# A transformer layer on one core: the state-space parameter chain placed between u's four projections, its loads put on three queues, and the attention mask filled by VectorE

## Chip, cores and metric

The kernel runs on one core of one Trainium2 chip. The metric is the device time of one launch in microseconds (us). Engines are TensorE (PE; its weight loads are shown as PEld), VectorE (DVE), ScalarE (ACT), GpSimd (POOL) and SyncE (SP, which here only issues DMAs). A "q" behind an engine's name is its instruction queue, from which it issues DMAs too.

## The reference, cut to what matters

One layer on 1024 tokens of width 1024, in float32:

```
proj = x @ w_in                      -> q | k | v | u, each 1024 x 512
a = differential attention(q, k, v)  4 heads, two score maps each, softmax over chunks of 64:
                                     token t sees keys of chunks <= its own chunk
s = diagonal complex state space on u: 32 groups x 16 channels, 64 states each
    lam_bar = exp(lam * exp(log_dt)); b_bar = (lam_bar - 1) / lam * b; y = Re(c h) + d u
    then gelu and a gated unit (w_glu)
h = LayerNorm(alpha x + [a, s] @ w_out)
y = LayerNorm(alpha h + mixture of 32 experts, two per token)
```

The parameters of the state space (a, log_dt, b, c) need a chain of small elementwise work before the first group of u can be used: exponentials, a sine and cosine, powers of lam_bar, and the rotated b and c.

## The kernel before

Float32 products are made from two float32r parts, a high part (ACT casts) and the rest (DVE subtracts), so that one projection of 128 output columns is 48 matmuls of 128x512 (`proj`, L221): three for each of eight k tiles and two token halves. Its weights go through one raw buffer (`load_w`, L188, an SP load into the area `misc`), then `split_w` (L209) makes two pairs of parts in the tiles wa and wb in turn. A projection's result is a pair of PSUM banks, of which there are two.

The order of the program is:

- x is loaded in eight parts on SP (L194 to L197, w_in's column tile 12 after the fourth), turned on PE and split (`turn_x`, L199).
- u's four projections, column tiles 12 to 15 (L264), each written to `u_dram` and read back as `UT` by eight SP loads (`proj_u`, L244).
- The parameter chain, L268 to L526: eleven small loads into `a_in`, `ea` and `lamv` on ACT's queue (L376 to L384); `a_in` is turned on PE (`pa`, L390) and copied to `aa` (L393); then two exponentials (`vexp`), sine and cosine (`vsincos`), the powers LR and LI (L410 to L428), the factors CR and CI, the squares UC and US (L448 to L458), all on DVE; b loaded (L467 to L470) and rotated into BB1 and BB2; c loaded (L484 to L486), turned (`pc`, L490) and negated into CA and CB; and the tables pl and ph (`phases`, L499). B's four and cin's four loads are on ACT's queue.
- Eight units of four groups (`ssm_pair`, L636). `ssm_prepare(u)` (L543) makes X (three GpSimd operations), turns it on PE (`pk`, `pw`, L566 and L567), and makes M and C on GpSimd and Sn on DVE. X has one buffer. `ssm_unit` (L595) runs the scan. Behind each unit stands one of the projections q0 to q3, v0 to v3 as filler for PE.
- k's four projections, then attention by 32 pairs (head, block of 128 queries), two started ahead (L893). `scores` (L772) makes for each of two maps the score products (L781, L782), adds the mask, takes the maximum (DVE, L792 or L799) and the exponential (ACT, L786); `weigh` (L803) combines the two maps on DVE and multiplies by v on PE (L815, L819).
- The mask: `negr` (1x128: -1e30 for the first 64 query rows, 0 for the others) times `oner` (1x64 of ones), added to the last 64 keys by one matmul with one contraction row (L783), for every map of every pair: 64 in all.
- The output product `mix` (L1071), routing, and 32 experts from L1337 on.

What sets the order: the framework schedules before the run. Each engine has one queue that runs in order. The framework fills these queues with a model of time of its own, and among the instructions whose inputs that model has ready it takes the one that stands first in the program; so the place in the program is a priority, and an instruction may stand in its queue before one that is earlier in the program. From the first expert's gather on, the program's own order is kept (`keep_order`, L1309). A tile that takes another's place in memory waits until the earlier one is done with: the tiles come from 25 slots handed out in turn (`Slots`). B1 gets the slot of one of x's raw tiles. `pa` is a tile of the PSUM bank that x's turns use as well (`bank`, L131).

Of the kernel before, what the change touches and what calls it, by code (L numbers as in the profile page):

```python
# [11 lines left out]
F32 = mybir.dt.float32  # L12
F32R = mybir.dt.float32r
# [6 lines left out]
P = 128  # L20
# [5 lines left out]
NG = 32  # L26
# [88 lines left out]
def tile_kernel(ctx: ExitStack, tc: tile.TileContext, I: dict, out: bass.AP, dbg=None):  # L115
# [9 lines left out]
    sl = Slots()  # L125
# [62 lines left out]
    def load_w(ct):  # L188
# [2 lines left out]
        SP.dma_start(r, w_in[:, ct * P:(ct + 1) * P].rearrange("(k p) n -> p k n", p=P))  # L191
        wraw[ct] = r

    for t_ in range(NT):  # L194
        SP.dma_start(xraw[t_ // 2][:, t_ % 2, :], x2[t_ * P:(t_ + 1) * P, :])
        if t_ == WPOS:
            load_w(12)  # L197
# [46 lines left out]
    def proj_u(c4):  # L244

        o = proj(12 + c4)
        ut = sl.get([P, 8, P], F32, f"ut{c4}")
        for half in range(2):
            S.copy(ut[:, :, half * 64:half * 64 + 64],
                   o[:, half * 512:half * 512 + 512].rearrange("p (b s) -> p s b", s=8))  # L250
        SP.dma_start(u_dram[c4], ut)
        sl.put(ut)
        if c4 % 2 == 0:
            UTs[c4 // 2] = sl.get([P, 2, 8, P], F32, f"UT{c4}")
        UT = UTs[c4 // 2][:, c4 % 2, :, :]
        for s_ in range(8):
            tau = 7 - s_
            SP.dma_start(UT[16 * tau:16 * tau + 16],
                         u_dram[c4].rearrange("(g c) s b -> s c g b", c=16)[s_])
# [1 line left out]
    UTs, zT, qr, vv = {}, {}, {}, {}  # L261


    for c4 in range(4):  # L264
        proj_u(c4)


    spp = Area(sl, 2, "ssmp")  # L268
    tmpp = Area(sl, 4, "ssmt")
    n_tmp = [0]  # L270
    KEPT = ("mag", "LR", "LI")

# [100 lines left out]
        return so, co  # L373


    a_in = tmpp.get("a_in", [4, 64], parts=NG)  # L376
    for j in range(2):
        PQ.dma_start(a_in[:, j, :], I["ssm_a_re"][0])
        PQ.dma_start(a_in[:, 2 + j, :], I["ssm_a_im"][0])
    ea = small(NG + 2, "ea", keep=True)  # L380
    PQ.dma_start(ea[:, 0:NG], I["ssm_log_dt"][0].partition_broadcast(P))
    lamv = tmpp.get("lamv", [4, 64])
    for j, nm in enumerate(("lam_q1", "lam_k1", "lam_q2", "lam_k2")):
        PQ.dma_start(lamv[:, j, :], I[nm][0].partition_broadcast(P))  # L384
    lamp = tmpp.get("lamp", [2, 64])
    mul(lamp, lamv[:, 0::2, :], lamv[:, 1::2, :])
    V.tensor_reduce(out=ea[:, NG:NG + 2], in_=lamp, axis=AX.X, op=ALU.add)
# [74 lines left out]

    BB1 = bigp("BB1", [P, NG, 16])
    BB2 = bigp("BB2", [P, NG, 16])
    B1 = sl.get([P, 4, 512], F32, "B1")
    b1, b2, b3, b4 = (B1[:, j, :].rearrange("p (g c) -> p g c", c=16) for j in range(4))
    PQ.dma_start(b1[0:64], I["ssm_b_re"][0].rearrange("g p c -> p g c"))  # L467
    PQ.dma_start(b1[64:P], I["ssm_b_im"][0].rearrange("g p c -> p g c"))
    PQ.dma_start(b2[0:64], I["ssm_b_im"][0].rearrange("g p c -> p g c"))
    PQ.dma_start(b2[64:P], I["ssm_b_re"][0].rearrange("g p c -> p g c"))  # L470
    ts(b2[0:64], b2[0:64], -1.0, ALU.mult)
    CRb = CR.unsqueeze(2).broadcast_to([P, NG, 16])
    CIb = CI.unsqueeze(2).broadcast_to([P, NG, 16])
# [6 lines left out]
    sl.put(B1)  # L480
    CA = bigp("CA", [P, NG, 16])
    CB = bigp("CB", [P, NG, 16])
    cin = sl.get([P, 2, 4, 2, 64], F32, "cin")
    for v, pair in enumerate((("ssm_c_re", "ssm_c_im"), ("ssm_c_im", "ssm_c_re"))):  # L484
        for j, nm in enumerate(pair):
            PQ.dma_start(cin[:, v, :, j, :], I[nm][0].rearrange("(t g) c p -> (g c) t p", t=4))  # L486
    for v, dst in ((0, CA), (1, CB)):
        pc = bank(f"pc{v}")
        for t_ in range(4):
# [35 lines left out]
    dump("CB", CB)  # L525
    dump("nlam", nlam)  # L526

    tmpp.close()

    areas = [Area(sl, 1, f"ssm{j}") for j in range(5)] + [misc]  # L530
# [151 lines left out]
    kk = {}  # L682
# [57 lines left out]
                sl.put(wgh, wgl, gl_["raw"])  # L740


    negr = cp.tile([1, P], F32R, name="negr")
    G.memset(negr.bitcast(F32)[:, 0:64], -1e30)
    G.memset(negr.bitcast(F32)[:, 64:P], 0.0)
    oner = cp.tile([1, 64], F32R, name="oner")
    G.memset(oner.bitcast(F32), 1.0)
    mhalf = cp.tile([P, 4], F32, name="mhalf")
    G.memset(mhalf, -0.5)
    gcol = cp.tile([P, 1], F32, name="gcol")  # L750
# [21 lines left out]
    def scores(h, i, qd, L, j):  # L772
        n = P * (i + 1)
        tk = slice(i * P, (i + 1) * P)
        p_ = sl.get([P, 2, T], F32, f"p{h}_{i}")
        nm = sm("nm", 2)

        def products(s_, c):
            for c0 in range(0, n, 512):
                w = min(512, n - c0)  # L780
                PE.matmul(s_[:, c0:c0 + w], qd[0][:, c, tk], kk[h][:, c, c0:c0 + w], start=True, stop=False)  # L781
                PE.matmul(s_[:, c0:c0 + w], qd[1][:, c, tk], kk[h][:, c, c0:c0 + w], start=False, stop=c0 + w < n)  # L782
            PE.matmul(s_[:, n - 64:n], negr, oner, start=False, stop=True)  # L783

        def weights(s_, c):
            S.activation(p_[:, c, 0:n], s_[:, 0:n], AF.Exp, bias=nm[:, c:c + 1], accum_out=L[:, j, c:c + 1])  # L786

        if n <= 512:
            s2 = bank2(f"s{h}_{i}").rearrange("p (c n) -> p c n", c=2)
            for c in range(2):  # L790
                products(s2[:, c, :], c)
            V.tensor_reduce(out=nm, in_=s2[:, :, 0:n], axis=AX.X, op=ALU.max, negate=True)  # L792
            for c in range(2):
                weights(s2[:, c, :], c)
        else:
            for c in range(2):
                s_ = bank2(f"s{h}_{i}_{c}")
                products(s_, c)
                V.tensor_reduce(out=nm[:, c:c + 1], in_=s_[:, 0:n], axis=AX.X, op=ALU.max, negate=True)  # L799
                weights(s_, c)  # L800
        return p_
# [720 lines left out]
```

## Time and profile before

| | |
|---|---|
| Median of 3 runs | 1197.9 us (1195.63 to 1200.3) |
| The profiled execution | 1199.21 us, span 1197.5 us |
| PE busy | 1078.5 us, 90% of the span |
| DVE busy | 972.9 us, 81% |
| ACT busy | 704.2 us, 59% |
| POOL busy | 358.3 us, 30% |
| Chain that ended last | PE 62% of the span, DVE 5%, DMA 2% |

The stages are, by the times at which their lines run: x and u 0 to 64 us; the state space with q, v and k's projections to about 270; attention to about 430; the output product and routing to about 570; the experts to about 1135; the second LayerNorm to the end. Busy time is that of an engine that has an instruction; PEclk is the share of full clock granted to TensorE: 1.00 is 2.4 GHz, 0.50 is 1.2 GHz. In a timeline, a bracket says how long the engine was idle before a row and what ended it.

### The profile page before, as it was taken

How to read it: one execution, taken by the hardware profiler on the slowest of the kernel's cores; microseconds unless marked ns; L12 is line 12 of the kernel's file. 1: busy time of each engine (PE TensorE's matmuls, PEld its weight loads, DVE VectorE, ACT ScalarE, POOL GpSimd, SP SyncE). 2: the span in 40 equal slices, each digit the busy share in tenths (PEclk: the TensorE clock that was granted, in tenths of full speed). 3: DMA queues.
4: the chain of work that ended last, by engine and by line, in shares of the span. 5: the costliest groups of instructions: out<-in, count | busy, mean ns of one | idle time of the engine just before them, and what ended most of it. 6: DMA issues, size and time to landing. Idle time of an engine off the chain costs nothing.

```text
span 1197.5 us, 15035 instructions
## 1 busy us (share of the span) xinstructions
PE 1078.5 (90%) x5313; PEld 898.3 (75%) x5313; DVE 972.9 (81%) x1410; ACT 704.2 (59%) x942; POOL 358.3 (30%) x279
## 2 busy tenths in 40 slices
PE   7987998898899989995999999999999999999900
PEld 5876787786678778884888888888888888888700
DVE  5598677646877674556999999999999999999958
ACT  3222334435666553213888888888888888888602
POOL 0058556422352453261122122112112212211024
PEclk9988999997999999995999999999999999999955
DMA  5641111201121355554699999999999999998076
GB/s 199 141 106 46 46 41 46 58 16 38 36 54 36 117 178 186 198 189 177 235 362 383 376 380 390 384 392 385 383 384 360 388 380 377 401 379 319 21 279 187
DMA packets 89213, 271.01 MB, mean 226 GB/s; under 512 B 30128, under 2 KB 50608, under 8 KB 64688
## 3 DMA queue, kind: packets, MB, share of 16 engines
q1 hardware_dynamic: 65968, 245.18, 54.5%
q0 software_dynamic: 11216, 23.61, 6.8%
q10 hardware_dynamic: 11952, 1.23, 0.8%
q8 instruction: 43, 0.70, 0.2%
q14 instruction: 34, 0.28, 0.1%
HBM read 254.12 MB, written 27.26 MB: 235 GB/s over the span
## 4 chain that ended last, share of the span: by engine, by line
PE 62%; DVE 5%; DMA 2%; issue 1%; ACT 1%; SPq 0%; DVEq 0%; POOL 0%; ACTq 0%; POOLq 0%
PE g L1239 14%; PE y L1230 14%; PE u L1239 14%; PE mix L1071 7%; PE xT L1201 3%; PE po L819 2%; PE glu L729 2%; DMA mo<-moe_dram 2%; PE hT L1213 1%; PE pl L1093 1%; PE s L781 1%; PE at L815 1%; PE s L782 1%; DVE mo L161 1%; PE hT L1089 1%
## 5 line engine op out<-in xcount | busy, mean ns | idle before, releaser
L1140 POOL DMA_INDIRECT moe_dram<-yo,idx x32 | 54.0, 1687 | 445.3 <-DVE yo L164 430.2
L233 PE MATMUL proj<-xh,wa 128*128 128x512 f32 x256 | 75.9, 403 | 1.8 <-ACT ssm L674 1.6
L233 PE MATMUL proj<-xh,wb 128*128 128x512 f32 x256 | 75.7, 408 | 1.6 <-ACT ssm L674 1.6
L1071 PE MATMUL mix<-woh,mx 128*128 128x512 f32 x256 | 73.2, 396 | 1.6 <-DVE mx L155 1.6
L1135 POOL DMA_INDIRECT gx<-h_dram,idx x32 | 60.2, 1880 | 24.0 <-DVE WT L161 14.6
L786 ACT ACTIVATE p<-s,nm 128x1024 f32<-128x1024 f32 (+7 forms) x64 | 47.2, 742 | 26.1 <-DVE nm L799 19.5
L233 PEld LDWEIGHTS proj<-xh,wb 128*128 128x128 f32 x256 | 49.5, 196 | 12.1 <-ACT ssm L674 1.8
L233 PEld LDWEIGHTS proj<-xh,wa 128*128 128x128 f32 x256 | 48.5, 193 | 11.9 <-ACT ssm L674 1.8
L1071 PEld LDWEIGHTS mix<-woh,mx 128*128 128x128 f32 x256 | 47.2, 188 | 11.2 <-DVE mx L155 2.1
L1246 ACT ACTIVATE yo<-y,WT 128x1024 f32<-128x1024 f32 (+1 forms) x33 | 35.9, 1092 | 28.0 <-PE y L1230 27.4
L781 PE MATMUL s<-kk,qh 128*128 128x512 f32 (+3 forms) x96 | 41.8, 435 | 11.3 <-ACT p L786 10.2
L799 DVE TENSOR_REDUCE nm<-s 128x1 f32<-128x1024 f32 (+3 forms) x32 | 32.6, 1020 | 14.3 <-PE s L783 14.3
L1201 PEld LDWEIGHTS xT<-ident,gx 128*128 128x128 f32 x256 | 36.0, 206 | 10.1 <-DMA gx<-h_dram,idx 6.0
L1201 PE MATMUL xT<-ident,gx 128*128 128x128 f32 x256 | 36.7, 286 | 7.2 <-DMA gx<-h_dram,idx 5.8
L233 PE MATMUL proj<-xl,wa 128*128 128x512 f32 x128 | 42.9, 405 | 0.0
L155 DVE TENSOR_TENSOR xe<-xT,xe 128x1024 fp32r<-128x1024 f32 (+1 forms) x33 | 39.1, 1186 | 4.4 <-ACT xe L174 4.4
L164 DVE SCALAR_TENSOR_TENSOR yo<-gx,first,yo 128x1024 f32<-128x1024 f32 (+1 forms) x33 | 41.3, 1253 | 1.5 <-ACT yo L1246 0.8
L819 PE MATMUL po<-vv,half 128*128 128x128 f32 x288 | 42.3, 287 | 0.0
L233 PE MATMUL proj<-xl,wb 128*128 128x512 f32 x128 | 42.1, 404 | 0.0
L1071 PE MATMUL mix<-wol,mx 128*128 128x512 f32 x128 | 41.6, 394 | 0.0
L174 ACT CAST xe<-xT 128x1024 fp32r<-128x1024 f32 (+1 forms) x33 | 32.3, 978 | 13.7 <-PE xT L1201 13.7
L819 PEld LDWEIGHTS po<-vv,half 128*128 128x128 f32 x288 | 36.6, 195 | 1.8 <-ACT half L816 0.4
(862 smaller groups left out, 3527.7 us busy)
## 6 DMA issues: line engine op xcount, KB each, us to landing
misc<-in_w_in_dram SPq DMA_DIRECT2D x16, 512.0 KB, 4.1
mo<-moe_dram SPq DMA_DIRECT2D x11, 512.0 KB, 9.2
xr<-in_x_dram SPq DMA_DIRECT2D x8, 512.0 KB, 6.7
wo_raw<-in_w_out_dram SPq DMA_DIRECT2D x4, 1024.0 KB, 4.9
xa<-in_x_dram SPq DMA_DIRECT2D x8, 512.0 KB, 4.6
h_dram<-xa SPq DMA_DIRECT2D x8, 512.0 KB, 4.7
out_dram<-mo SPq DMA_DIRECT2D x8, 512.0 KB, 3.0
mo<-moe_dram POOLq DMA_DIRECT2D x5, 512.0 KB, 12.2
```

The lines of the kernel that those rows point to most:

```text
L155: eng.tensor_tensor(out=out_, in0=a, in1=b, op=ALU.subtract)
L164: return V.scalar_tensor_tensor(out=out_, in0=a, scalar=s, in1=b, op0=op0, op1=op1)
L233: PE.matmul(o[:, hs], wt[kt // 4][:, w_, kt % 4, :], x_[:, hs], start=(kt == 0 and n == 0), stop=(kt == KT - 1 and n == 2))
L781: PE.matmul(s_[:, c0:c0 + w], qd[0][:, c, tk], kk[h][:, c, c0:c0 + w], start=True, stop=False)
L786: S.activation(p_[:, c, 0:n], s_[:, 0:n], AF.Exp, bias=nm[:, c:c + 1], accum_out=L[:, j, c:c + 1])
L819: PE.matmul(po[:, j * P:(j + 1) * P], aT[:, k, :], vv[k // 4][:, k % 4, h * P:(h + 1) * P], start=(k == 0), stop=(k == i))
L1071: PE.matmul(o[-(hs.start > 0)][:, hs], mx[:, m_, kt, :], (woh, wol)[w_][kt // 2][:, kt % 2, hs], start=(kt == 0 and n == 0), stop=(kt == K ...
L1135: return G.indirect_dma_start(out=dst, out_offset=None, in_=h_dram[:, :], in_offset=bass.IndirectOffsetOnAxis(ap=ix, axis=0), bounds_check ...
L1140: G.indirect_dma_start(out=moe_dram[:, :], out_offset=bass.IndirectOffsetOnAxis(ap=ix, axis=0), in_=src, in_offset=None, bounds_check=2 * ...
L1201: PE.transpose(b_[:, kt * P:(kt + 1) * P], rows(g_, kt), ident)
L1230: PE.matmul(y[:, hs], hid[e][:, x_, kt, :], w_[:, k, hs], start=(kt == 0 and n == 0), stop=(kt == 3 and n == 2))
L1239: PE.matmul(o, xT[e][:, x_, kt, :], w_[:, k, :], start=(kt == 0 and n == 0), stop=(kt == KT - 1 and n == 2))
```

## The change

The parameter chain is moved in the program. Its eleven small loads go ahead of x's loads (a's four on ACT's queue; log_dt and lamv's four on POOL's), and B's and cin's eight loads go onto SP's queue behind u's first projection and behind the load of column tile 13. The chain itself stands behind u's first projection; the second comes ahead of b's rotation, the third ahead of c's turn, the fourth behind the tables. The mask matmul and its constants go; a DVE memset writes -1e30 over the same scores (48 memsets: one for both maps where a pair has up to 512 keys, else one for each map).

```diff
+    tmpp = Area(sl, 4, "ssmt")
+    a_in = tmpp.get("a_in", [4, 64], parts=NG)
+    ea = tmpp.get("ea", [NG + 2])
+    lamv = tmpp.get("lamv", [4, 64])
+    G.dma_start(ea[:, 0:NG], I["ssm_log_dt"][0].partition_broadcast(P))
+    for j in range(2):
+        S.dma_start(a_in[:, j, :], I["ssm_a_re"][0])
+        S.dma_start(a_in[:, 2 + j, :], I["ssm_a_im"][0])
+    for j, nm in enumerate(("lam_q1", "lam_k1", "lam_q2", "lam_k2")):
+        G.dma_start(lamv[:, j, :], I[nm][0].partition_broadcast(P))
     for t_ in range(NT):
         SP.dma_start(xraw[t_ // 2][:, t_ % 2, :], x2[t_ * P:(t_ + 1) * P, :])
...
-    for c4 in range(4):
-        proj_u(c4)
+    proj_u(0)
+    load_w(13)
...
     spp = Area(sl, 2, "ssmp")
-    tmpp = Area(sl, 4, "ssmt")
+    B1 = sl.get([P, 4, 512], F32, "B1")
+    b1, b2, b3, b4 = (B1[:, j, :].rearrange("p (g c) -> p g c", c=16) for j in range(4))
+    SP.dma_start(b1[0:64], I["ssm_b_re"][0].rearrange("g p c -> p g c"))
+    SP.dma_start(b1[64:P], I["ssm_b_im"][0].rearrange("g p c -> p g c"))
+    SP.dma_start(b2[0:64], I["ssm_b_im"][0].rearrange("g p c -> p g c"))
+    SP.dma_start(b2[64:P], I["ssm_b_re"][0].rearrange("g p c -> p g c"))
+    cin = sl.get([P, 2, 4, 2, 64], F32, "cin")
+    for v, pair in enumerate((("ssm_c_re", "ssm_c_im"), ("ssm_c_im", "ssm_c_re"))):
+        for j, nm in enumerate(pair):
+            SP.dma_start(cin[:, v, :, j, :], I[nm][0].rearrange("(t g) c p -> (g c) t p", t=4))
...
     BB1 = bigp("BB1", [P, NG, 16])
     BB2 = bigp("BB2", [P, NG, 16])
-    B1 = sl.get([P, 4, 512], F32, "B1")
...
+    proj_u(1)
     ts(b2[0:64], b2[0:64], -1.0, ALU.mult)
...
-    cin = sl.get([P, 2, 4, 2, 64], F32, "cin")
...
+    proj_u(2)
     for v, dst in ((0, CA), (1, CB)):
...
+    proj_u(3)
     tmpp.close()
...
-    negr = cp.tile([1, P], F32R, name="negr")
-    G.memset(negr.bitcast(F32)[:, 0:64], -1e30)
-    G.memset(negr.bitcast(F32)[:, 64:P], 0.0)
-    oner = cp.tile([1, 64], F32R, name="oner")
-    G.memset(oner.bitcast(F32), 1.0)
...
-                PE.matmul(s_[:, c0:c0 + w], qd[1][:, c, tk], kk[h][:, c, c0:c0 + w], start=False, stop=c0 + w < n)
-            PE.matmul(s_[:, n - 64:n], negr, oner, start=False, stop=True)
-
+                PE.matmul(s_[:, c0:c0 + w], qd[1][:, c, tk], kk[h][:, c, c0:c0 + w], start=False, stop=True)
...
+            V.memset(s2[0:64, :, n - 64:n], -1e30)
             V.tensor_reduce(out=nm, in_=s2[:, :, 0:n], axis=AX.X, op=ALU.max, negate=True)
...
+                V.memset(s_[0:64, n - 64:n], -1e30)
                 V.tensor_reduce(out=nm[:, c:c + 1], in_=s_[:, 0:n], axis=AX.X, op=ALU.max, negate=True)
```

## Rows read from the trace of the kernel before

**Rows 1.** The page: the chain that ended last, by engine.

```profile
PE 62%; DVE 5%; DMA 2%; issue 1%; ACT 1%; SPq 0%; DVEq 0%; POOL 0%; ACTq 0%; POOLq 0%
```

**Rows 2.** Windows of 6 us: PE, PEld, DVE, ACT, POOL busy, then PEclk, DMA share, GB/s.

```profile
72.00:78.00 6.00, 3.76 (x17) 2.79 (x15) 5.90 (x10) 1.14 (x2) 6.00 (x5) 1.00 0.89 169
78.00:84.00 6.00, 4.93 (x19) 4.36 (x20) 5.76 (x14) 1.82 (x3) 3.44 (x3) 0.53 0.05 6
84.00:90.00 6.00, 6.00 (x29) 5.02 (x28) 5.83 (x11) 0.00 (x0) 3.47 (x3) 0.90 0.01 3
90.00:96.00 6.00, 2.46 (x11) 1.69 (x9) 5.93 (x6) 0.00 (x0) 5.84 (x5) 0.96 0.05 10
96.00:102.00 6.00, 4.59 (x19) 4.21 (x20) 5.09 (x8) 0.00 (x0) 5.69 (x5) 0.50 0.39 105
102.00:108.00 6.00, 5.69 (x27) 4.40 (x26) 5.26 (x6) 3.06 (x7) 3.63 (x4) 0.97 0.00 0
108.00:114.00 6.00, 3.87 (x34) 3.48 (x33) 5.73 (x8) 1.53 (x3) 5.92 (x3) 1.00 0.07 14
```

**Rows 3.** Waits of PE, 0 to 300 us: total us, times, longest.

```profile
PE pk L566 <- POOL ssm L161: 9.4, 3, 4.9
```

**Rows 4.** Timelines of DVE, PE and POOL: start us, us; the chain's start, middle, ends.

```profile
31.34 0.69 DVE L155 TENSOR_TENSOR xl<-xT,xh 128x512 fp32r<-128x512 f32 x1 [0.26 <-ACT xh L174]
...
42.15 0.31 PE L390 MATMUL pa<-ident,ssmt 32*128 32x32 f32 x2
...
45.28 0.22 DVE L393 COPY ssmt<-pa 128x64 f32<-128x64 f32 x1
...
61.54 0.69 DVE L158 TENSOR_TENSOR B<-B,ssmt 128x512 f32<-128x512 f32 x1
62.14 0.22 DVE L158 TENSOR_TENSOR ssmt<-LR 128x64 f32<-128x64 f32 x1
...
73.21 0.28 DVE L161 TENSOR_TENSOR LI<-ssmt 128x128 f32<-128x128 f32 x1
...
88.33 0.28 DVE L161 TENSOR_TENSOR ssmp<-ssmt,ssmt 128x128 f32<-128x128 f32 x1
...
95.76 1.59 POOL L161 TENSOR_TENSOR ssm<-ssm 128x512 f32<-128x512 f32 x1
```

**Rows 5.** The same timelines: ACT and PE at the start, ACT's DMA issues.

```profile
8.51 1.11 PE L205 MATMUL xT<-ident,xr 128*128 128x128 f32 x4 [0.23 <-DMA xr<-in_x_dram]
...
10.77 2.05 ACT L174 CAST xh<-xT 128x512 fp32r<-128x512 f32 x4 [8.05 <-DMA ssmt<-in_ssm_log_dt_dram]
...
20.85 1.14 ACT L174 CAST wb<-misc 128x512 fp32r<-128x512 f32 x2 [3.05 <-DMA misc<-in_w_in_dram]
...
29.98 0.69 ACTq L467 DMA_DIRECT2D B<-in_ssm_b_re_dram  x1
...
37.65 0.53 ACTq L486 DMA_DIRECT2D cin<-in_ssm_c_re_dram  x1
```

**Rows 6.** PE's timeline: products of one map, its mask, the next map's first product.

```profile
340.01 0.39 PE L781 MATMUL s<-kk,qh 128*128 128x512 f32 x1
340.24 0.40 PE L782 MATMUL s<-kk,ql 128*128 128x512 f32 x1
340.56 0.29 PE L783 MATMUL s<-oner,negr 1*128 1x64 f32 x1
340.79 0.50 PE L781 MATMUL s<-kk,qh 128*128 128x512 f32 x1
```

**Rows 7.** Attention's window, of L783 alone (PE, PEld) and of all; columns as in rows 2.

```profile
290.00:408.90 118.90, 14.99 (x50) 9.36 (x50) 0.97 0.16 43
...
290.00:408.90 118.90, 113.28 (x660) 92.22 (x659) 91.12 (x156) 72.38 (x146) 48.52 (x36) 0.97 0.16 43
```

**Rows 8.** A DVE memset, and an expert stretch's window; columns as in rows 2.

```profile
0.86 0.09 DVE L412 MEMSET LR<- 128x32 f32 x1 [0.86 <-PEq L1511]
...
700.00:730.00 30.00, 30.00 (x140) 25.00 (x139) 29.39 (x27) 24.97 (x28) 7.41 (x4) 1.00 1.00 387
```

More of the change, by code (lines that the diff above doesn't have):

```diff
@@ L373, in vsincos @@
         return so, co
[L376 to L384, printed above, removed]
     lamp = tmpp.get("lamp", [2, 64])
@@ L464, in tile_kernel @@
     BB2 = bigp("BB2", [P, NG, 16])
-    B1 = sl.get([P, 4, 512], F32, "B1")
[L466 to L470, printed above, removed]
+    proj_u(1)
     ts(b2[0:64], b2[0:64], -1.0, ALU.mult)
@@ L482, in tile_kernel @@
     CB = bigp("CB", [P, NG, 16])
-    cin = sl.get([P, 2, 4, 2, 64], F32, "cin")
-    for v, pair in enumerate((("ssm_c_re", "ssm_c_im"), ("ssm_c_im", "ssm_c_re"))):
-        for j, nm in enumerate(pair):
-            PQ.dma_start(cin[:, v, :, j, :], I[nm][0].rearrange("(t g) c p -> (g c) t p", t=4))
+    proj_u(2)
     for v, dst in ((0, CA), (1, CB)):
```

## The prediction

> **What bounds the kernel now.** I read the page's chain of waits first: of the chain that ended last, PE is 62% and no other engine over 5% [rows 1]. The expert stage, more than half of the span, shows PE busy 30.00 of 30 us at full clock with DVE at 29.39 [rows 8]; the change does not touch it, so whatever is won or lost before it shifts it as a whole. What counts is PE's lost time ahead of the experts, so I looked next at the windows for places where PE has holes or half clock, then at PE's waits for their cause.
>
> The first such place is 72 to 114 us, where the state space starts [rows 2]. PE's holes there, 6 less its busy time in each row, sum to 2.24 + 1.07 + 0 + 3.54 + 1.41 + 0.31 + 2.13 = 10.7 us. Two of the windows also run near the lower of the two clock levels, 1.2 GHz (granted 0.53 and 0.50), each behind a hole of 2 us or more in the row before. Busy time times the missing share of the clock gives what that costs: 4.93 x 0.47 + 6.00 x 0.10 + 2.46 x 0.04 + 4.59 x 0.50 + 5.69 x 0.03 = 5.5 us. Together 16.2 us. Of the holes, 9.4 us in three waits are PE's `pk` waiting for GpSimd's X [rows 3]. X needs the powers and the rotated b, so this goes back to the parameter chain. The chain's timeline shows the reader that its work is not slow but late: `a_in` has been loaded since the start, yet `pa` runs on PE at 42.15 and its copy on DVE at 45.28, because all four of u's projections have priority over it; the last power is done at 73.49, the last table at 88.61, and the X of the second unit on GpSimd at 97.35 [rows 4].
>
> The second place is attention. Between 290 and 408.9 us PE is busy 113.28 of 118.9 us, DVE 91.12 [rows 7]: PE is the bound, DVE 77% full.
>
> **The change part by part.**
>
> *The chain earlier.* Its place before the second projection lets `pa` go when its PSUM bank is free. That bank serves x's turns, whose last parts leave DVE at 31.34 + 0.69 = 32.0 [rows 4]; so the copy to `aa` falls at about 32 in place of 45.3: **13 us earlier**. DVE's chain then runs beside projections on PE. The splits of the later weights now stand behind it in priority. They need not wait for it: in the present trace a rotation of b, of lower priority, runs at 61.54 ahead of a power at 62.14 [rows 4], since each chain step leaves gaps in which a ready instruction goes ahead. What stands behind X on GpSimd is M and C, and C needs the tables; those come 13 us earlier as well, so X of the second unit ends near 84 in place of 97.35. What is late next is PE itself, with a projection per unit as cover. The gain lies between 3 us (the first wait alone goes) and the 16.2 us that are lost there; the shift caps it at 13, and I take **12**, as DVE will meet one or two splits whose weights have not landed.
>
> *Small loads ahead of x, on ACT and POOL.* ACT's first cast starts at 10.77, behind its own DMA issues, while the matmuls it needs start at 8.51 and take 1.11 us [rows 5], ending at 9.6. With four issues left on ACT the cast can go then: 10.77 - 9.62 = **1.2 us won**, at worst none. POOL has nothing else to do there. The two lam sums on DVE wait for POOL's loads; they feed only `ea`, and the first weight split stands in the same queue, so a late load could hold it: none to 2 us, I take none because the present load came on a queue that x's loads held up.
>
> *B and cin on SP.* ACT loses eight issues, from 29.98 to 38.18 [rows 5], which hid under projections: nothing won. On SP they stand by the program behind the load of tile 13, but their slots are free from the start while that load must wait for the raw buffer, so they can go ahead of it: up to 38.18 - 29.98 = 8.2 us of issue in front of a weight that now lands by 20.85 [rows 5]. u's read-back and all later weight loads queue behind the same instructions. Until x's second half is through, PE can use that tile as filler; a loss of none to 5 us, I take **1** since x's own turns and the first projection's second half cover most.
>
> *The mask.* Removed: 64 matmuls, one for each of 4 heads, 8 blocks and 2 maps. The price of one is read from starts in [rows 6]: two 512-column products stand 340.24 - 340.01 = 0.23 us apart, but the mask comes 340.56 - 340.24 = 0.32 behind the second (0.09 more), and holds the next product for another 340.79 - 340.56 = 0.23. So 0.32 each, 20.5 us of PE in all. Fifty lie in the PE-bound stretch [rows 7], 16 us; the other fourteen lie before and behind it, where the loop through maximum and exponential sets the pace. "TensorE: Matmul & The Clock Gate" of the Trainium skill (Back-to-back issue gap) has pairs of weight load and matmul at about 81 ns for 128 columns; by that the mask would be worth at most 64 x 0.081 = 5.2 us and the change's sum would be some 5 us smaller. The trace has four times that price, and the trace decides.
>
> Added: 48 memsets on DVE, 16 over both maps and 32 over one, on the path from the products to the maximum, where the mask matmul was. No row shows a memset of PSUM. The nearest are a memset in SBUF, 0.09 us [rows 8], and a copy out of PSUM, 0.22 [rows 4]; below nothing is excluded, since it is an instruction more. I take 0.15, between the two because it is a memset by kind and touches PSUM: 48 x 0.15 = 7.2 us of DVE (4.3 to 10.6). The latency of the path stays as it is: 0.32 on PE goes, 0.15 and a hand-over come. "VectorE: DVE Perf Modes" (The TRN2 errata) has a fixed term of about 150 cycles at 0.96 GHz for an operation; by that one would cost, as an estimate, some 0.22 us at 64 elements and the sum would be at most 48 x 0.07 = 3.4 us worse; no row here shows it.
>
> What DVE then holds: 48 x 50/64 = 38 memsets in the stretch, 91.1 + 5.7 = 97 us, against PE's 113.3 - 16 = 97. If the full 16 us went, the stretch would be 103 us long and both engines 94% full, with ACT's exponentials between them; then the maximum, and behind it the freeing of the score banks, is late next. I credit 9 of the 16 us, and 1 of the rest: **10 us**. Bounds: 1 and 20.5.
>
> *Sum:* 1.2 - 1 + 12 + 10 = 22 to 23 us, against the profiled execution's 1199.2 (1.3 above the median of the runs): **1176 us**.
>
> **The rivals.**
>
> *VectorE bounds attention.* Holes of DVE behind PE's products fill, but each maximum now starts after a memset, and DVE's combining of the two maps stands in the same queue. Then the mask is worth 2 us: 1199.2 - 12 - 2 = **1185**. For it: the two 97s above. Against: 28 us of DVE are idle in the stretch now.
>
> *The wait moves to GpSimd.* Nine operations per unit remain there, and in 90 to 102 us it is busy 11.5 of 12 us [rows 2]. If that, and not the chain, holds X of the second unit, only the first wait goes with its half clock (3 + 2 us), the mask stays worth 10, the queues nothing: **1184**. It includes the case that the move changes less than it says because the framework sets the order. Against: from 78 to 90 us GpSimd is busy only 3.44 and 3.47 of 6 us [rows 2] while DVE still makes the tables that C waits for, so it is itself late by the chain.
>
> *The chain stands in front of the weights (slower).* If DVE's queue holds the splits of tiles 13 to 15 behind the chain's steps, PE has no operands: the chain up to the tables takes 88.6 - 45.3 = 43 us, from 32 to 75, and only then comes tile 15; with its 48 x 0.23 = 11 us and the 11 of q0, PE stands only at 97 where it now stands at 72 + 3.76 = 76 [rows 2], u's projections and q0 done: 21 us lost, and three more holes cost half clock as above, 7 us. Won back are the waits for X, 10, and, with DVE fuller, 10 from the mask: **1207**. It decides from the point where a split comes more than some 5 us after its weight has landed. Against it is the interleaving shown at 61.54.
>
> *All of it comes.* 16.2, 1.2 and 18 of the mask: **1164**.
>
> **How the numbers follow.** My forecast 0.50, VectorE as bound 0.14, GpSimd 0.13, the chain before the weights 0.13, all of it 0.10. A measurement of this kernel can tell about 0.5%, 6 us, from no change. The forecast's own range is 1166 to 1188; to hold eight in ten it takes in 1164 on the one side and the two cases at 1184 and 1185 with their spread to 1196 on the other, but not 1207. Faster by over 0.5%: the forecast, all of it, and most of the cases at 1184 and 1185, together 0.77; within 0.5%: 0.10, from these two where B, cin or the memset cost their upper ends; slower: 0.13.
>
> **What would show it.** Right: `pa` near 32 us; the last table near 75; no wait of `pk` for GpSimd over 1 us and no half clock between 72 and 114; no L783; between the start of attention and `mix` some 10 us less with PE still over 93% busy; the experts' stretch as before and only shifted. The memset's mean shows the price. Wrong: holes of PE at 24 to 30 us (tile 13 late behind B and cin), at 42 to 64 (splits behind the chain), or PE waiting in attention for the maximum with DVE above 95%. If `pa` still runs after 40 us, the move did nothing.

## The result and the profile after

The changed kernel takes **1185.8 us** (median of 5 executions, 1185.2 to 1189.3) against 1197.9 of the kernel before on the same chip: ratio 0.9892, 95% interval 0.9874 to 0.9910, so 12 to 13 us faster. On another chip, in one of the sets of experiments below, it was 0.9912 (0.9888 to 0.9936). The profiled execution took 1186.1 us, span 1184.3.

The page's chain that ended last, of after; PE's share grew from 62 to 73% [rows 1], DVE's from 5 to 12%:

```profile
PE 73%; DVE 12%; DMA 6%; ACT 4%; issue 2%; SPq 2%; POOL 1%; DVEq 0%; ACTq 0%; POOLq 0%
```

The windows of [rows 2], of after; the columns are the same:

```profile
72.00:78.00 6.00, 5.80 (x30) 4.61 (x28) 5.83 (x14) 0.00 (x0) 2.28 (x3) 1.00 0.07 29
78.00:84.00 6.00, 0.00 (x0) 0.00 (x0) 5.97 (x5) 0.00 (x0) 5.92 (x4) 0.86 0.16 41
84.00:90.00 6.00, 4.03 (x17) 3.64 (x18) 5.91 (x8) 1.42 (x3) 5.69 (x5) 0.50 0.33 91
90.00:96.00 6.00, 6.00 (x25) 4.91 (x24) 5.90 (x5) 0.03 (x1) 5.50 (x5) 0.78 0.29 74
96.00:102.00 6.00, 5.09 (x40) 4.52 (x39) 4.72 (x8) 3.58 (x7) 3.98 (x2) 1.00 0.03 5
102.00:108.00 6.00, 6.00 (x29) 4.98 (x28) 4.33 (x5) 1.15 (x2) 5.84 (x5) 1.00 0.40 109
108.00:114.00 6.00, 6.00 (x29) 4.91 (x28) 5.84 (x7) 0.62 (x1) 5.27 (x5) 1.00 0.09 19
```

PE's holes add up to 0.20 + 6.00 + 1.97 + 0 + 0.91 + 0 + 0 = 9.1 us, and the clock, which is granted at 0.50 behind the long hole, costs 4.03 x 0.50 + 6.00 x 0.22 = 3.3 us: 12.4 in place of 16.2. Several small holes became one large one, from 78 to 84, with DVE and GpSimd full in it. PE's waits from 0 to 300 us name it (total, times, longest):

```profile
PE xT L216 <- DMA xr<-in_x_dram: 8.9, 3, 5.0
...
PE pk L570 <- POOL ssm L161: 8.2, 1, 8.2
PE py L628 <- DVE ssm L155: 3.8, 2, 2.8
```

The wait for X is still there, 8.2 us in one piece where it was 9.4 in three [rows 3]. Yet the chain came earlier, as the timelines of PE, DVE and GpSimd show:

```profile
33.25 0.31 PE L401 MATMUL pa<-ident,ssmt 32*128 32x32 f32 x2
...
35.20 0.21 DVE L404 COPY ssmt<-pa 128x64 f32<-128x64 f32 x1
...
61.46 0.29 DVE L161 TENSOR_TENSOR LI<-ssmt 128x128 f32<-128x128 f32 x1
...
62.46 1.21 DVE L155 TENSOR_TENSOR ssmp<-ssmt,ssmt 128x256 f32<-128x256 f32 x1
...
77.41 0.39 PE L244 MATMUL proj<-xh,wa 128*128 128x512 f32 x1
...
77.52 0.28 DVE L161 TENSOR_TENSOR ssmp<-ssmt,ssmt 128x128 f32<-128x128 f32 x1
...
84.19 1.72 POOL L161 TENSOR_TENSOR ssm<-ssm 128x512 f32<-128x512 f32 x1
...
85.97 0.61 PE L570 MATMUL pk<-ssmp,ssm 128*128 128x16 f32 x2 [8.17 <-POOL ssm L161]
```

Against [rows 4] the copy to `aa` is 10.1 us earlier, the last power 11.8, the last table 10.8, X of the second unit 11.4. But PE reaches `pk` of the second unit at 77.8 and stands there until 85.97, in the middle of q0. The start, in SP's and ACT's timelines:

```profile
12.64 0.76 SPq L282 DMA_DIRECT2D B<-in_ssm_b_re_dram  x1
...
12.81 2.06 ACT L174 CAST xh<-xT 128x512 fp32r<-128x512 f32 x4 [8.66 <-DMA gcol<-in_subln_g_dram]
...
26.65 0.51 SPq L289 DMA_DIRECT2D cin<-in_ssm_c_re_dram  x1
...
27.27 7.21 SPq L191 DMA_DIRECT2D misc<-in_w_in_dram  x2
...
32.14 1.14 ACT L174 CAST wb<-misc 128x512 fp32r<-128x512 f32 x2 [1.86 <-DMA misc<-in_w_in_dram]
```

ACT's first cast is 2.0 us later than in [rows 5], and tile 13's cast 11.3 us later, since all eight loads of B and cin are issued ahead of its load. VectorE's queue stops for B as well: a negation on b stands in it ahead of x's next splits and waits 2.68 us for its load, and PE's transposes then wait for a split:

```profile
25.86 0.42 DVE L168 TENSOR_SCALAR B<-B 64x512 f32<-64x512 f32 x1 [2.68 <-DMA B<-in_ssm_b_im_dram]
...
27.86 0.66 PE L216 MATMUL xT<-ident,xr 128*128 128x128 f32 x4 [0.66 <-DVE xl L155]
```

In the mask's place the trace has these groups on VectorE (ns minimum, median, maximum):

```profile
L797 DVE MEMSET s<- x32: 112/112/112, 267.9 to 378.1; 64x64 f32 x32
...
L789 DVE MEMSET s<- x16: 165/165/165, 274.8 to 410.2; 64x128 f32 x16
```

Attention, from its first product to the first `mix`, in one window each (columns of [rows 2]). Before, and after:

```profile
268.20:422.20 154.00, 142.25 (x784) 115.00 (x785) 113.67 (x196) 94.39 (x197) 56.95 (x44) 0.92 0.21 60
```

```profile
266.80:410.70 143.90, 116.44 (x723) 100.84 (x721) 117.36 (x242) 93.54 (x196) 54.13 (x42) 0.96 0.21 63
```

Read so: PE's work at full clock is busy time times granted clock, 130.9 us before and 111.8 after: **19 us of work gone**. Its holes are length less busy time, 11.8 before and 27.5 after: **16 us came back as waiting**. The remaining 6 to 7 us of the 10.1 by which this stage is shorter are half clock: 11.4 us lost before, 4.7 after. Such losses vary between executions of one kernel: of the 18 executions of before beside the first set of experiments the fastest, 1194.7 us, had a mean granted clock of 0.949, the slowest, 1204.5, one of 0.941. So one profile doesn't price the mask; the experiments do.

### The profile page after: what moved, and what is told of

Same layout as the page of the kernel before. It is cut to its first block, busy times and chain, and to the rows that moved or that the text cites. A ratio compares the mean times of both kernels' runs of the same rounds, so it can differ in the third digit from the quotient of the medians.

```text
span 1184.3 us, 14997 instructions
## 1 busy us (share of the span) xinstructions
PE 1051.2 (89%) x5249; PEld 884.4 (75%) x5249; DVE 977.9 (83%) x1458; ACT 703.6 (59%) x942; POOL 361.0 (30%) x281
## 4 chain that ended last, share of the span: by engine, by line
PE 73%; DVE 12%; DMA 6%; ACT 4%; issue 2%; SPq 2%; POOL 1%; DVEq 0%; ACTq 0%; POOLq 0%
PE g L1238 15%; PE y L1229 14%; PE u L1238 14%; PE proj L244 8%; PE mix L1070 7%; PE xT L1200 3%; DMA misc<-in_w_in_dram 2%; DMA mo<-moe_dram 2%; PE po L818 1%; PE glu L733 1%; PE hT L1212 1%; PE s L780 1%; DVE ssmt L158 1%; PE pl L1092 1%; ACT p L783 1%
## 5 line engine op out<-in xcount | busy, mean ns | idle before, releaser
L783 ACT ACTIVATE p<-s,nm 128x1024 f32<-128x1024 f32 (+7 forms) x64 | 47.1, 741 | 23.3 <-DVE nm L798 14.0
L244 PEld LDWEIGHTS proj<-xh,wb 128*128 128x128 f32 x256 | 48.7, 194 | 11.7 <-ACT ssm L678 2.0
L780 PE MATMUL s<-kk,qh 128*128 128x512 f32 (+3 forms) x96 | 36.9, 389 | 18.6 <-ACT p L783 15.4
L174 ACT CAST xe<-xT 128x1024 fp32r<-128x1024 f32 (+1 forms) x33 | 32.3, 978 | 13.6 <-PE xT L1200 13.6
L174 ACT CAST wa<-misc 128x512 fp32r<-128x512 f32 x16 | 9.8, 620 | 47.2 <-DMA misc<-in_w_in_dram 41.9
## 6 DMA issues: line engine op xcount, KB each, us to landing
mo<-moe_dram POOLq DMA_DIRECT2D x5, 512.0 KB, 11.9
```

The costliest lines, as they stand in the source:

```text
L174: S.copy(hi, raw)
L244: PE.matmul(o[:, hs], wt[kt // 4][:, w_, kt % 4, :], x_[:, hs], start=(kt == 0 and n == 0), stop=(kt == KT - 1 and n == 2))
```

## The experiments

They ran in four sets, each set on a chip of its own beside executions of the kernel before (medians 1197.9 to 1199.3 us); ratios are to these, with 95% intervals. The changed kernel itself ran in one of these sets only, the one with the memset twice, without it, and with X on VectorE. Runs of the other sets are compared with it by their ratios, and between its first result, 0.9892, and its second, 0.9912, lie 2.4 us. Where the code for one and for two maps changes alike, a diff shows one of the two; "..." stands for what is left out.

**One part alone.** First the kernel before with VectorE's mask:

```diff
-            PE.matmul(s_[:, n - 64:n], negr, oner, start=False, stop=True)
...
+                V.memset(s_[0:64, n - 64:n], -1e30)
```

> The kernel before with the mask by VectorE alone; the chain and all loads as before. Theory 1 (the mask gave nearly the whole gain, the weave about 1 us): 1187 us, between 1185 and 1190, first mix some 10 us earlier than before's and the space from 0 to 268 us as in before. Theory 2 (the mask gives its 10 us only because the weave delivers q, k and v or z earlier, so that alone it is worth less): 1191 or more.

Measured 1193.7 us, ratio 0.9957 (0.9941 to 0.9973): the mask alone is worth 5 us, half of what was expected. Its attention window:

```profile
267.90:416.50 148.60, 121.75 (x721) 104.47 (x721) 118.85 (x243) 93.60 (x196) 54.66 (x44) 0.92 0.22 63
```

The work is 112.0 us and the holes 26.9, as in the changed kernel; only the clock is that of before. Theory 1's 1187 failed; the number is theory 2's. Then the changed kernel with the mask matmul back:

```diff
+            PE.matmul(s_[:, n - 64:n], negr, oner, start=False, stop=True)
...
-                V.memset(s_[0:64, n - 64:n], -1e30)
```

> The changed kernel with the mask matmul on PE again. Theory 1 (the weave moves the chain 11 us earlier, but PE pays about as much at the start and in the wait for X of the second unit): 1196 to 1197, so 1 to 2 us faster than before. Theory 2 (parts of the weave are worth the 12 us of the prediction but the mask gave nothing in return): 1186.

Measured 1193.7 us, 0.9948 (0.9925 to 0.9971): 6 us for the weave (the chain and its loads moved in between the projections), between the two theories. Both theories fell, the second's reason too: the mask gains the same with and without the weave. The third theory, 6 and 5, went into the next run, the changed kernel unchanged:

> The changed kernel itself, beside the kernel before on the chip of this set. Theory 3 (the weave gives about 6 us and the mask about 5; a single execution's half-clock stretches in attention come and go by some 5 us from run to run): ratio 0.989 to 0.991, 1186 to 1189 us. Theory 4 (the changed kernel's attention escaped a half-clock stretch only on the first chip): ratio 0.993 to 0.995 like the runs that do one part alone, 1191 to 1193 us.

Measured 1189.8 us, 0.9912 (0.9888 to 0.9936). The executions run from 1183.3 us (mean clock 0.951) to 1190.9 (0.944), so this chip reaches the times of the first result too. The profile's attention:

```profile
266.50:414.60 148.10, 121.45 (x722) 105.69 (x721) 118.07 (x243) 94.08 (x198) 54.44 (x42) 0.92 0.21 62
```

The same work (111.7) and holes (26.7) as in the first profile, with a loss to half clock of 9.7 in place of 4.7. Theory 3 is the nearer one, if just beyond its range.

**What the memset costs.** Each memset twice:

```diff
             V.memset(s2[0:64, :, n - 64:n], -1e30)
+            V.memset(s2[0:64, :, n - 64:n], -1e30)
```

> The changed kernel with each of the 48 memsets done twice: 6.2 us more work on VectorE, nothing else. If VectorE's queue (memset, maximum, combining of the maps) is what PE waits for in attention: 5 to 7 us slower than the changed kernel, 1191 to 1194 us. If the memset is a small part of a loop of products, maximum, exponential and free bank that runs beside other heads' work: at most 2 us slower, 1186 to 1189 us.

Measured 1193.0 us, 0.9962 (0.9941 to 0.9983), against 0.9912 of the changed kernel in the same set: 3 us by the medians, 6 by the ratios, for 6.2 us of work. It is not hidden, which is the first of the two cases. And no memset:

```diff
-            V.memset(s2[0:64, :, n - 64:n], -1e30)
```

> The changed kernel without the memsets: the causal mask of the diagonal blocks is left out altogether. If VectorE's queue is what PE waits for: 5 to 7 us faster than the changed kernel, 1180 us. If not: 0 to 2 us faster, 1184 to 1187 us, and PE's holes between the first score and mix stay near the 27 us that they are with the memset.

Measured 1175.8 us, 0.9816 (0.9794 to 0.9838): 11.5 us less than the changed kernel by the ratios, 14 by the medians, about twice the memsets' own time and more than either case had. Its attention window:

```profile
264.90:397.80 132.90, 115.22 (x722) 100.07 (x720) 111.46 (x195) 92.80 (x196) 55.14 (x41) 0.96 0.24 68
```

The work is the same 110.6 us; the holes fall to 17.7. The same from the other side, the kernel before without any mask:

```diff
-            PE.matmul(s_[:, n - 64:n], negr, oner, start=False, stop=True)
```

> The kernel before without any mask: the mask matmul is taken away and nothing put in its place, so the causal mask of the diagonal blocks is left out. If the 19.5 us of PE are worth nearly their length on the path as long as nothing takes their place: 1179 to 1183 us, attention some 133 us long, PE's holes in it near 17. Then the memset, which is the difference to the run with the mask by VectorE alone (ratio 0.996), costs 10 to 14 us and not its own 6.2. If the memset costs about its own length: 1186 to 1188 us.

Measured 1181.7 us, 0.9861 (0.9839 to 0.9882), with these holes (17.2):

```profile
268.50:406.00 137.50, 120.30 (x722) 104.84 (x722) 112.67 (x196) 93.67 (x198) 56.32 (x44) 0.92 0.24 68
```

Five of these runs and the kernel before make one table of ratios:

| | mask on PE | mask on VectorE | no mask |
|---|---|---|---|
| chain and loads as before | 1 | 0.9957 | 0.9861 |
| weave | 0.9948 | 0.9912 | 0.9816 |

Down each column the weave is worth 0.45 to 0.52%, 5 to 6 us of 1199. Along the rows the matmul's removal is worth 1.3 to 1.4%, 16 to 17 us, and the memset takes back 0.96% in both, 11.5 us. A single difference here is uncertain by some 3 us, and the cells come from three sets. With the changed kernel's first ratio, 0.9892, in its cell the weave would be worth 0.65% beside VectorE's mask and the memset would take back 0.76%. So each part alone is worth about 4 to 8 us, and the memset takes back 9 to 12.

Where does the memset lose more than its own time? In VectorE's timeline of after another instruction often stands between it and its maximum:

```profile
301.10 0.11 DVE L797 MEMSET s<- 64x64 f32 x1
301.13 0.67 DVE L164 SCALAR_TENSOR_TENSOR p<-p,rho 128x512 f32<-128x512 f32 x1
301.72 0.80 DVE L798 TENSOR_REDUCE nm<-s 128x1 f32<-128x640 f32 x1
```

So it is for 28 of the 48 pairs, and the time from a memset's end to its maximum adds up to 13.2 us. A run tied the two together:

```diff
-            V.memset(s2[0:64, :, n - 64:n], -1e30)
-            V.tensor_reduce(out=nm, in_=s2[:, :, 0:n], axis=AX.X, op=ALU.max, negate=True)
+            with tc.tile_critical():
+                V.memset(s2[0:64, :, n - 64:n], -1e30).then_inc(msem, 1)
+                mcnt[0] += 1
+                V.wait_ge(msem, mcnt[0])
+                V.tensor_reduce(out=nm, in_=s2[:, :, 0:n], axis=AX.X, op=ALU.max, negate=True)
```

> The changed kernel with memset and maximum tied together, so that no other instruction of VectorE stands between them (in the changed kernel something stands between 28 of the 48 pairs, and the gaps add up to 13 to 14 us). The tie costs an empty instruction and a jump on VectorE for each pair. Theory 7 (the memset costs twice its own time because the maximum then waits behind other work): gaps under 2 us in all, 3 to 8 us faster than the changed kernel, 1179 to 1185 us. Theory 8 (only VectorE's amount of work counts): no faster than the changed kernel, 1186 us or, by the jumps, more.

Measured 1300.1 us, 1.0854. The ties work, the maximum follows 0.04 us behind, but VectorE stands still in front of every tie, 111 us over the 48; one of them:

```profile
301.27 0.11 DVE L802 MEMSET s<- 64x64 f32 x1 [1.17 <-PE at L821]
301.42 0.96 DVE L805 TENSOR_REDUCE nm<-s 128x1 f32<-128x768 f32 x1
```

The price of the tie, over 100 us for 48, hides the question: inconclusive. The next run took the work off VectorE altogether:

```diff
-            V.memset(s2[0:64, :, n - 64:n], -1e30)
             V.tensor_reduce(out=nm, in_=s2[:, :, 0:n], axis=AX.X, op=ALU.max, negate=True)
+            S.activation(s2[0:64, :, n - 64:n], s2[0:64, :, n - 64:n], AF.Copy, bias=-1e30, scale=0.0)
```

> The changed kernel with the masked cells written by ScalarE between the maximum and the exponential; the maximum then runs over unmasked scores, which leaves the softmax as it is. VectorE loses 6.2 us of memsets and the gaps behind them, ScalarE, 65% busy in attention, gains 48 writes of perhaps 0.2 us. If the memset's cost lies in VectorE's queue: 4 to 9 us faster than the changed kernel, 1178 to 1183 us. If it lies in the loop from products to free bank, which ScalarE's writes lengthen as well: 1186 to 1192 us.

Measured 1188.7 us, 0.9926 (0.9905 to 0.9946): not faster, as the second case had it. VectorE is relieved (115.5 us against 118.1), ScalarE has 102.3 against 94.1, and PE's waits change their kind; its longest, one that VectorE ends, and the window:

```profile
PE s L780 <- ACT p L783: 19.0, 13, 3.7
...
PE at L814 <- DVE p L164: 2.0, 1, 2.0
```

```profile
266.50:413.10 146.60, 120.98 (x723) 104.67 (x721) 115.48 (x194) 102.25 (x245) 57.37 (x42) 0.92 0.21 62
```

The holes, 25.6 us, are as long as with VectorE's mask. PE waits for the exponential that frees a pair of score banks, and there are two pairs (`bank_pair`); but it also waits for VectorE itself. PE's waits over the whole of attention, before and in the changed kernel:

```profile
PE s L781 <- ACT p L786: 10.2, 8, 3.4
```

```profile
PE s L780 <- ACT p L783: 15.4, 13, 3.3
PE at L814 <- DVE s L797: 3.9, 1, 3.9
PE s L780 <- DVE p L164: 2.9, 1, 2.9
PE at L814 <- DVE p L164: 2.5, 2, 1.3
```

Added up by what ended them (us), for this and the other runs:

| attention of | all holes | scores, ended by the exponential | ended by VectorE |
|---|---|---|---|
| before | 11.8 | 10.2 | 0 |
| before, no mask | 17.2 | 11.6 | 3.4 |
| changed kernel, no mask | 17.7 | 11.4 | 3.9 |
| before, VectorE's mask | 26.9 | 13.6 | 11.7 |
| changed kernel, first and second profile | 27.5, 26.7 | 15.4, 14.7 | 10.3, 10.5 |
| changed kernel, memset twice | 28.9 | 18.5 | 7.2 |
| changed kernel, ScalarE's mask | 25.6 | 19.0 | 3.2 |

As the profile has it, of the 9 to 10 us of holes that the memset adds in the changed kernel 6 to 7 are waits that VectorE ends and 3 to 4 are waits for the exponential. With ScalarE's mask the first kind falls back to 3.2 and the second grows to 19.0. The equal sum is thus not one and the same wait. It fits the reading that a step put anywhere between products and free pair of banks lengthens that loop, and VectorE's load alone doesn't explain it; but the load's part is not excluded, and no run with a third pair of banks tests the loop itself.

**Where the chain's 11 us went.** First the loads of the start: the small ones (one of them shown) back behind the first projection on ACT, and slots of x's raw tiles for B and cin, so that SP takes tile 13 first.

```diff
-    G.dma_start(ea[:, 0:NG], I["ssm_log_dt"][0].partition_broadcast(P))
...
+    S.dma_start(ea[:, 0:NG], I["ssm_log_dt"][0].partition_broadcast(P))
...
+    sl.free.rotate(-2)
     B1 = sl.get([P, 4, 512], F32, "B1")
...
+    sl.free.rotate(2)
```

> The changed kernel with the small parameter loads again behind the first projection on ACT, and B and cin given slots of x's raw tiles so that SP issues them behind the weight of tile 13. Theory 1 (loads at the start cost PE about 4 us, but PE's stock of projections is then used up as much earlier, so the wait for X of the second unit grows by what is saved): tile 13's weight cast near 20 us and projection 14 starting near 42.5 in place of 46.3, the wait of pk for GpSimd 11 to 12 us in place of 8.2, the total 1184 to 1186, hardly changed. Theory 2 (the start is a loss of its own): the wait stays at 8 us and the total is 1181 to 1182.

Measured 1189.8 us, 0.9913 (0.9880 to 0.9947): no gain against the changed kernel's 0.9912, and above both theories' times. The first projection starts at 14.1 in place of 16.4 and tile 13's cast is at 21.6, but projection 14 does not come at 42.5: it starts at 46.6, where it was 46.3. The gain is lost in between, as B still comes late for VectorE's queue:

```profile
26.01 0.42 DVE L168 TENSOR_SCALAR B<-B 64x512 f32<-64x512 f32 x1 [1.90 <-DMA B<-in_ssm_b_im_dram]
...
27.19 0.66 PE L210 MATMUL xT<-ident,xr 128*128 128x128 f32 x4 [1.94 <-DVE xl L155]
```

So this run doesn't undo the start's loss; it moves it. `pk` waits 5.5 us, where both theories had 8 or more. The first score is at 265.1, within the 264.3 to 266.8 of the seven profiles that have the changed kernel's code up to there. Then the order on GpSimd:

```diff
+        with tc.issue_after(xdone[max(u, 1)].ins):
+            combine(C, low(cL), high(cH), low(sL), high(sH), sub, G, "tb")
...
-    made[0] = ssm_prepare(0)
+    for u in range(2):
+        parts[u] = ssm_prepare(u)
+    made[0] = parts.pop(0) + ssm_prepare2(0)
```

> The changed kernel with X of the second unit traced and queued ahead of C of the first unit on GpSimd; same operations, other order. Theory 1 (PE's 8.2 us wait is a matter of order: X stands behind a C that waits for the last table): X of the second unit ends near 72 to 76 in place of 85.9, pk waits under 1 us, the window from 84 to 96 runs at full clock, the total is 1174 to 1179. Theory 2 (GpSimd's and VectorE's amount of work sets the pace of the first units, whatever the order): PE waits as long some operations later, for C or for the next X, total 1183 to 1186.

Measured 1191.7 us, 0.9930 (0.9907 to 0.9954). `pk` doesn't wait any more, but PE's longest wait is now another:

```profile
PE py L648 <- DMA ssm<-ssm: 12.0, 1, 12.0
```

That is the read of the small matrix Ks into Tm: its addition stands in VectorE's queue at 85.84, behind other work, its eight loads on SP from 87 to 96 with u's read-back between them, and PE has used up q0 and 13 products of q1 by then. Theory 1 had the end of `pk`'s wait, but not the time. Theory 2 had the wait that comes later, but for C or X and not for Ks, and 1191.7 lies above both ranges. That the amount of work sets the pace is so far argued. How much GpSimd slows VectorE's chain is the next question, tried by putting nine of GpSimd's operations onto VectorE:

```diff
-        combine(X, per_c(BB1), power(LR, 0), per_c(BB2), power(LI, 0), add, G, "tb")
+        combine(X, per_c(BB1), power(LR, 0), per_c(BB2), power(LI, 0), add, *((V, "tv") if u < 2 else (G, "tb")))
-        combine(M, per_c(CA), power(LR, 1), per_c(CB), power(LI, 1), add, G, "tb")
+        combine(M, per_c(CA), power(LR, 1), per_c(CB), power(LI, 1), add, *((V, "tv") if u < 1 else (G, "tb")))
```

> The changed kernel with X of the first two units and M of the first one computed by VectorE in place of GpSimd; nine operations of some 0.7 us more on VectorE, none on GpSimd between 60 and 71 us. Theory 5 (VectorE's steps of 0.2 us take 1.1 to 1.4 us whenever GpSimd runs beside them, and that, not the amount of work, holds the last table and X of the second unit): powers and tables end near 73 in place of 77.8, the wait of pk falls from 8.2 to 1 to 3 us, total 1180 to 1184. Theory 6 (VectorE is full from 40 to 97 us and any work added to it comes out as waiting): last table at 77 or later, the holes between 70 and 132 us as large as now, total 1186 to 1190.

Measured 1187.4 us, 0.9907 (0.9876 to 0.9938), not to be told from the changed kernel. The chain's step that took 1.21 us at 62.46 in after takes 0.43 here, though GpSimd has one operation open beside it, 5.86 us long. In the last run below, with GpSimd idle, it takes 0.41 (rows of VectorE, then of GpSimd):

```profile
63.46 0.43 DVE L155 TENSOR_TENSOR ssmp<-ssmt,ssmt 128x256 f32<-128x256 f32 x1
...
61.21 5.86 POOL L158 TENSOR_TENSOR ssm<-ssmp,LR 128x512 f32<-128x512 f32 x1 [2.91 <-DMA u_dram<-ut]
```

```profile
65.11 0.41 DVE L155 TENSOR_TENSOR ssmp<-ssmt,ssmt 128x256 f32<-128x256 f32 x1
...
75.17 2.22 POOL L158 TENSOR_TENSOR ssm<-ssmp 128x512 f32<-128x512 f32 x2 [10.53 <-DVE ssmp L155]
```

In the run at hand the chain's slow steps from 62 to 71 us are gone, and `pk` waits 2.8 us in all. But the last table ends at 76.4, not 73 (and at 78.8 in the last run), and the next wait grows:

```profile
PE py L628 <- DVE ssm L155: 8.3, 3, 6.4
```

So the slow steps of theory 5 are real, but that they hold the last table is not shown: VectorE's added work takes their place, as theory 6 had it, and the time is theory 6's. The last run took both edits:

> The changed kernel with both edits that removed a loss one by one: the loads of the start put back behind x and tile 13, and X of the first two units and M of the first on VectorE. If the two losses are separate: 3 to 5 us less than the changed kernel, 1181 to 1185 us, ratio to before near 0.987. If what is saved at the start or in the wait for X comes back as the next wait for VectorE (the wait of py for the scans): no faster than either alone, 1186 to 1189 us, ratio 0.990 to 0.992.

Measured **1184.0 us** (1182.9 to 1187.5), 0.9890 (0.9869 to 0.9912). The stretch from 70 to 132 us, in after and in this run:

```profile
70.00:132.00 62.00, 50.08 (x245) 42.12 (x245) 50.22 (x69) 14.79 (x26) 43.47 (x31) 0.89 0.20 56
```

```profile
70.00:132.00 62.00, 55.25 (x292) 46.47 (x291) 50.14 (x69) 18.71 (x32) 41.77 (x30) 0.97 0.22 60
```

The holes fall from 11.9 to 6.8 us and the loss to half clock from 5.5 to 1.7; the first score is at 261.7, 6.5 us ahead of before where the changed kernel is 1.4 ahead (1.7 in its second profile). The time is in the first theory's range, the ratio between the two. The median is the lowest of the runs that do all the work, but the ratio is that of the changed kernel's first result, 0.9892: that the total gains is not shown, only that the state space does.

## Why the prediction was right, and where it was not

The direction, the range (1164 to 1196) and "faster by over 0.5%" held. The sum did not: 22 us were forecast (22.2 off the 1199.2 that it names gives 1177, not 1176), 12 to 13 measured. The two large terms were each about twice too big: 12 for the chain with its loads, and 10 for the mask, came out near 5 to 6 and 5.

- **Small loads, 1.2 us won: lost instead.** ACT was freed of its issues, but the x tiles came later: from issue to landing the median is 9.1 us, before 6.7, beside the small loads from ACT and GpSimd; with these put back it is 6.8. PE's transposes of [rows 5], 8.51 before, run at 12.30, and the cast 2.0 us later. The step took ACT's queue for the limit and gave the transfers nothing.
- **B and cin on SP, 1 us lost: nearer 2, and partly by another wait.** They do go ahead of tile 13, whose load is issued at 27.27 (15.63 before), and as forecast x's turns fill PE in the meantime, but for a hole of 0.66 us between 24 and 30. Projection 14 starts 3.8 us later in all, 2.0 of which are the start's. What the sum left out is that a step on B stands in VectorE's queue ahead of x's splits; with the loads put back it takes what the start gives, and projection 14 stays at 46.6.
- **The chain earlier, 12 us: failed.** The shift was right (13 expected, 10 to 12 found from `aa` to X). The step that failed is "What is late next is PE itself, with a projection per unit as cover". PE's queue holds `pk` of the second unit earlier too: after 29 of q0's 48 products, where before all of q0 and 34 products of q1 stand in front of it. So PE met the later parts of the same work, and the hole moved with the chain. What is late next was VectorE, busy 96% or more in each 6 us from 60 to 90, with GpSimd's X behind it, and then Ks and the scans. The rival of a wait moved to GpSimd was the nearest: it left the second wait standing, and its 1184 is as near the result as the other rival's. Of the weave's 5 to 6 us, 2.4 are there at the first score: it is at 265.8 on average (264.3 to 266.8) in the seven profiles with the changed kernel's code up to it, at 268.2 (267.9 to 268.5) in three of before's. From the last `mix` product to the end the same profiles differ by 1.5 us on average (661.8 and 663.3), with ranges that overlap. Where the rest lies is open; single profiles differ too much in attention's clock.
- **The mask.** Its price on PE was right: 20.5 us expected, 19 found, and 16 to 17 on the time when nothing takes its place. "TensorE: Matmul & The Clock Gate" of the Trainium skill (Back-to-back issue gap), by which it would have been worth at most 5.2 us, doesn't fit this matmul: the two runs without a mask gain three times that. The memset's own price was right as well: 0.15 estimated, 0.112 and 0.165 measured, 6.2 us in all for 7.2. "VectorE: DVE Perf Modes" of the Trainium skill (The TRN2 errata), whose fixed term is measured on copies and additions there and by which a memset would be, as an estimate, some 0.22 us at 64 elements, is above both; the measurement decides. What failed is the sentence "The latency of the path stays as it is" and the credit of 9 of 16 from both engines being 94% full: on the path from the products to a free pair of banks the memset costs some 9 to 12 us, not its own 6.2.
- **VectorE bounds attention:** partly. In the window that answers to [rows 7], shifted by the 1.4 us, DVE is at 98 of 119, where the forecast had 97 of 103, and PE at 100.6:

```profile
288.60:407.50 118.90, 100.55 (x632) 86.84 (x630) 98.04 (x198) 76.16 (x158) 50.98 (x39) 0.99 0.20 62
```

Neither engine is full. That rival had the result, 1185, and part of its mechanism is in the rows: over 10 us of PE's waits in attention end with VectorE, 3 to 4 where it writes no mask. But taking the mask off VectorE gained nothing, and the rival also had 12 us for the chain.
- **The chain in front of the weights** did not come: PE is busy all of 42 to 64 us, though a step on B did stand in front of x's splits.

Of what was to show it right, `pa` near 32 us (33.25), the last table near 75 (77.8), no mask matmul, and attention 10 us shorter came in the first profile; PE over 93% busy in attention (81%: 116.4 of 143.9 us) and an absence of `pk` waits over 1 us and of half clock did not.

## What to carry to other kernels

Moving a chain earlier gains only what the consumer's queue holds as filler behind it: ask what PE meets next, and whether the engine that feeds it has slack, before crediting the shift. Put a load's first user where the load will have landed: in a queue that runs in order it holds whatever stands behind it. Work taken off the busiest engine, here 16 to 17 us, is worth its length only if nothing is put on the dependent steps around it in its place; a new step there can cost more than its own time (here 9 to 12 us for 6.2 on VectorE, and no less when ScalarE did it). And price a small gain by runs of each part alone and of both, beside each other: here one profile showed 10 us for a part that is worth about 5.

## What the runs showed of the hardware

VectorE's small steps can get several times longer while GpSimd works: the 128x256 addition took 1.21 us beside GpSimd and 0.41 with GpSimd idle, a 128x32 one 0.98 against 0.22. The extra, some 0.8 us, is more than half of a GpSimd operation, most of them 1.16 to 1.47 us there. It goes the other way too: a GpSimd operation took 5.86 us beside VectorE's steps, of which the 128x256 one then took 0.43. "SBUF — State Buffer" of the Trainium skill (SBUF: two separate sides) has a port pair that VectorE, in an operation with two inputs in SBUF, and GpSimd can only have in turn, each for a whole instruction while the other blocks; these rows agree.

A memset of PSUM by VectorE took 0.112 us for 64x64 and 0.165 us for 64x128 elements; the same cells written by ScalarE took 0.20 and 0.25 us. Tying two VectorE instructions together made attention 255 us long in place of 148, 2.2 us for each of the 48 ties; that includes the half clock, granted 0.77 on average there against 0.92.
